# A state-space stage in a new order, its tables' products one tile later, and two transposes moved

## The chip, the cores and the metric

The kernel runs on one core of a Trainium2 chip. The metric is the device time of one execution in microseconds (us). Engines: PE (matmul), PEld (its weight loads), DVE, ACT, POOL, and SP, which in this kernel only issues DMAs.

## The reference, cut to what matters

A network on x of 512 tokens by 1024 features, in float32. First two blocks, each a token mixer (two branches of softmax attention, gated) and a feed-forward layer; then a block with a state-space mixer and a convolutional feed-forward layer; then one with stick-breaking attention and the same layer. The two parts that the change touches:

```python
def token_mixer(u, ...):
    ...
    ya = blocked_attention(qa, ka, va, 1.0 / math.sqrt(GQA_HEAD_DIM))
    ...
def s5_mixer(h, w_in, a_re, a_im, log_dt, b_re, b_im, c_re, c_im, d_skip, w_glu):
    u = (h @ w_in).astype(f32).reshape(bsz, seq, N_GROUPS, SSM_GROUP)
    ...
    bu_re = jnp.einsum('blgh,gph->blgp', u, bb_re)
    ...
    _, _, s_re, s_im = lax.associative_scan(combine, (a_seq_re, a_seq_im, bu_re, bu_im), axis=1)
    y = (jnp.einsum('blgp,ghp->blgh', s_re, c_re) - jnp.einsum('blgp,ghp->blgh', s_im, c_im)
         + d_skip.astype(f32) * u)
    y = jax.nn.gelu(y.reshape(bsz, seq, D_SSM))
    z = y @ w_glu
    return z[..., :D_MODEL] * jax.nn.sigmoid(z[..., D_MODEL:])
```

The operators ab, bb and f come from the parameters alone, not from x.

## The kernel before, in words

Activations lie transposed, 128 features by 512 tokens a tile. Each float32 operand is split into a high and a low part, and a product is three matmuls of 128x512 (`wh` with both parts of x, `wl` with the high one); a weight tile of 512 KB is loaded to `raw` by SP (L199) and split by ACT (`wh`, L238) and DVE (`wl`, L241 or L255). The time line: mixer 0, feed-forward 0, mixer 1 (to about 1120 us), feed-forward 1 (`ffn1`, to about 1545), the state-space stage (`ssm`, to about 1700), `ffn2`, stick attention, `ffn2`.

**Plan.** Each stage adds functions to a plan, whose items are run in turn and record instructions; a scheduler then sets each engine's order by its own estimates, except for what is pinned in the order of the program.

**Mixer 1.** The table `MIX` sets the order of items: `f` and `g` are pieces of projections (six matmuls), and for attention `aq` scores (`s`), `ae` exponentials (`p`, L827), `an` the scaling of `p` by its sum (DVE, L834), `at` four transposes (`pT`, L367) with `pt` copied by ACT (L847) and its low part taken by DVE (L848), `ap` the product with v (`o`). `mixer` moves two items of it for l = 1.

**Tables.** `ssm_gen` returns a list of functions that `ffn1` of l = 1 spreads evenly over its items. For each of 8 tiles of groups, `gen(i)` has: `fetch` (SP loads `g_c` and `g_b`), `bbar` (`g_bb`), `stacks` (`g_bs`, and `g_c` scaled and copied, L1465 to L1468), `expansion` twice (the products of c and of bb with powers of the transition: L1425, L1426, and the sums `go` and `gw`, L1430, all DVE), `table(i)` (`gt`, L1405 to L1409), `lags` (PE products of `g_bs` with `g_c` and `go` into `gps`, and the stores of `go` to `od` and `g_gs` to `gg`), `flip` (PE transposes of `gw`, the store to `wd`) and `spread` (eight copies from `gg` to `td`). So the stage's operators `od`, `td`, `wd` and tables `cd` lie in DRAM.

**State-space stage.** After three leading tiles of u, the table `ORDER` gives the order of everything; all of it is pinned, on every engine. `u3.0` to `u7.3` are pieces of six matmuls for the u tiles; for tile i: E takes u from PSUM (DVE), A stores it to `ud` on ACT's queue (L1548), D loads it back rearranged as `U` on SP's (L1552), w, x, b and o load `wt`, `tt`, `tab` and `ot` on SP's (L1556 to L1568), S are the states (`vps`, eight small products that the trace shows as 16 matmuls), V, R, C, X and Z rotate, scan and turn them, T and O are the lags and the outs (both into `yps`), G, g, H, I the gelu, J, Q, a, l the way of y through DRAM, and k the matmuls of w_glu. `hi`, `lo` and `raw` stand for a weight's split and load. A DMA issue on SP or ACT that has to wait holds back what stands behind it on that engine.

Of the kernel before, what the change touches and what calls it, by code (L numbers as in the profile page):

```python
# [52 lines left out]
for _name, _w in (("ident", 128), ("ones_d", 128), ("ones_q", 128), ("ones_kv", 128), ("blk", 128),  # L53
# [4 lines left out]


ORDER = """  # L60
    o1 u3.0 o0 o4 o2 u3.1 b1 b0 M0 b4 b2 u3.2 M1 E1 u3.3 E0 A1 E2 hi u4.0 A0 E3 A2 u4.1 lo A3 u4.2 raw D1 u4.3 D0 E4
    hi u5.0 D2 D3 lo A4 u5.1 raw S1 u5.2 V1 o3 D4 S0 R1 u5.3 V0 w4 C1 S2 hi R0 M3 X1 u6.0 o6 E5 V2 T1 C0 A5 R2 M2 u6.1
    o5 X0 S4 Z1 C2 b3 u6.2 V4 x4 D5 Z0 M4 T0 X2 lo b6 u6.3 w6 R4 raw T2 hi E6 u7.0 w5 C4 A6 S3 Z2 M6 X4 lo b5 u7.1 o7
    V3 Z4 raw O1 b7 u7.2 G1 R3 w7 O0 g1 D6 H1 I1 J1 u7.3 C3 G0 x6 T4 g0 hi x5 x7 E7 Q1 M5 lo H0 S6 A7 X3 I0 raw S5 J0
    Z3 a1 V6 l1 O4 V5 O2 G4 R6 g4 D7 H4 T3 I4 G2 Q0 J4 g2 H2 T6 R5 Q4 a0 O3 C6 C5 X6 l0 X5 Z6 S7 M7 G3 Z5 a4 T5 V7 l4
    g3 O6 R7 H3 I2 C7 J2 O5 G6 I3 X7 g6 Q2 J3 Z7 H6 I6 T7 G5 J6 g5 Q3 H5 k0 a2 I5 l2 J5 Q6 a3 O7 l3 Q5 a6 l6 k1 G7 g7
    a5 H7 l5 I7 k2 J7 k3 Q7 k4 a7 l7 k5 k6 k7
"""


# [38 lines left out]
class Kernel:  # L109
# [4 lines left out]
    V0 = 20  # L114
    VD = 1
    O1 = 1
    O2 = 1
    RP = True
    PA = True
    H0 = 17  # L120
    Q1 = 'scalar'
    Q2 = 'sync'
    Q3 = 'scalar'
    Q4 = 'sync'
# [15 lines left out]
    S1 = (2,4)  # L140
# [756 lines left out]
    def mixer(self, l, xs, st, nxt, mid, feed=None):  # L897
# [252 lines left out]
            ops[f"y{p}"] = (lambda p=p: reload_y(p)), ()  # L1150
        mix = MIX.split()
        if l == 1:
            for x, y in (("aq0", "f13"), ("ae0", "f14")):
                mix.remove(x)
                mix.insert(mix.index(y) + 1, x)
        for x in mix:
# [112 lines left out]
    def ssm_gen(self):  # L1269
# [6 lines left out]
        g = {}  # L1276
# [113 lines left out]
        def table(i):  # L1390

            box = {}
            sh = [128, 8, 8, 8]
            gs_ = slice(8 * i, 8 * i + 8)
            H = lambda z: g["hi" + z][:, :, gs_].rearrange("p j g -> p g j").unsqueeze(3).to_broadcast(sh)
            L = lambda z: g["lo" + z][:, :, gs_].rearrange("p k g -> p g k").unsqueeze(2).to_broadcast(sh)

            def part(k, a, b, op):
                def f():
                    if k == 0:  # L1400
                        box["t"] = self.s4("gt", F32)
                    o = box["t"][:, k].rearrange("p (g j k) -> p g j k", g=8, j=8)
                    w = self.s2("cx")
                    x = w.rearrange("p (g j k) -> p g j k", g=8, j=8)
                    v.tensor_tensor(o, H("r"), L(a), ALU.mult)  # L1405
                    v.tensor_tensor(x, H("i"), L(b), ALU.mult)
                    v.tensor_tensor(box["t"][:, k], box["t"][:, k], w, op)
                    if k == 1:
                        nc.sync.dma_start(self.Cd[i], box["t"])  # L1409
                return f  # L1410
            return [part(0, "r", "i", ALU.subtract), part(1, "i", "r", ALU.add)]

        def expansion(out, c1, c2, a):

            sh = [128, 4, 8, 16]
            C = lambda c, k: c()[:, 4 * k:4 * k + 4].unsqueeze(2).to_broadcast(sh)
            P = lambda n, k: g[n][:, a:a + 8, g["g0"] + 4 * k:g["g0"] + 4 * k + 4].rearrange("p d g -> p g d").unsqueeze(3).to_broadcast(sh)
            res = []
            for k in range(2):
                box = {}  # L1420

                def mul(k=k, box=box):
                    o = out()[:, 4 * k:4 * k + 4].rearrange("p g (d h) -> p g d h", d=8)
                    t = box["t"] = self.s2("cx").rearrange("p (g d h) -> p g d h", g=4, d=8)
                    v.tensor_tensor(o, C(c1, k), P("P1", k), ALU.mult)  # L1425
                    v.tensor_tensor(t, C(c2, k), P("P2", k), ALU.mult)  # L1426

                def add(k=k, box=box):
                    o = out()[:, 4 * k:4 * k + 4].rearrange("p g (d h) -> p g d h", d=8)
                    v.tensor_tensor(o, o, box["t"], ALU.add)  # L1430
                res += [mul, add]
            return res

        def gen(i):
            box = {}
            gs_ = slice(8 * i, 8 * i + 8)

            def fetch():
                g["g0"] = 8 * i
                c = box["c"] = T("g_c", [2, 8, 16], 2)  # L1440
                b = box["b"] = T("g_b", [2, 8, 16], 2)
                nc.sync.dma_start(c, self.ins["ssm_c"][i])
                nc.sync.dma_start(b, self.ins["ssm_b"][i])

            def bbar():

                b = box["b"]
                bb = box["bb"] = T("g_bb", [2, 8, 16], 2)
                x = T("g_x", [8, 16])
                y = T("g_y", [8, 16])  # L1450
                F = lambda n: g[n][:, gs_].unsqueeze(2).to_broadcast([128, 8, 16])
                v.tensor_tensor(bb[:, 0], b[:, 0], F("fr"), ALU.mult)
                v.tensor_tensor(x, b[:, 1], F("fi"), ALU.mult)
                v.tensor_tensor(bb[:, 1], b[:, 1], F("fr"), ALU.mult)
                v.tensor_tensor(y, b[:, 0], F("fi"), ALU.mult)
                v.tensor_tensor(bb[:, 0], bb[:, 0], x, ALU.subtract)
                v.tensor_tensor(bb[:, 1], bb[:, 1], y, ALU.add)

            def stacks():

                bb, c = box["bb"], box["c"]
                bs = box["bs"] = T("g_bs", [8, 16], 2)
                v.tensor_copy(bs[up], bb[up, 0])
                v.tensor_copy(bs[dn], bb[dn, 1])
                v.tensor_scalar(c[dn], c[dn], -1.0, None, ALU.mult)  # L1465
                c0 = box["c0"] = T("g_c0", [8, 16], 2)
                v.tensor_copy(c0[up], c[up, 0])
                v.tensor_copy(c0[dn], c[dn, 1])  # L1468
                box["o"] = self.s4("go", F32, [128, 8, 128])
                box["w"] = self.s4("gw", F32, [128, 8, 128])  # L1470

            def lags():
                o, c0 = box["o"], box["c0"]
                bs = box["bs"].rearrange("p g h -> p (g h)")
                nc.sync.dma_start(self.Od[i], o)
                ps = self.ps("gps")
                for q in range(4):
                    r = slice(32 * q, 32 * q + 32)
                    for two in range(2):
                        z = 128 * two  # L1480
                        self.mm(ps[r, z:z + 16], bs[:, r], c0[:, 2 * q + two], start=True, stop=True)
                        self.mm(ps[r, z + 16:z + 128], bs[:, r], o[:, 2 * q + two, 0:112], start=True, stop=True)
                gs = T("g_gs", [128], 2)
                par = self.const("par")
                nc.scalar.activation(gs, ps[:, 0:128], AF.Copy, scale=par[:, 0:1])
                v.scalar_tensor_tensor(gs, ps[:, 128:256], par[:, 1:2], gs, op0=ALU.mult, op1=ALU.add)
                dd = T("g_dd", [16])
                v.tensor_tensor(dd, g["d"][:, 16 * i:16 * i + 16], self.const("delta"), ALU.mult)
                v.tensor_tensor(gs[:, 0:16], gs[:, 0:16], dd, ALU.add)
                nc.sync.dma_start(self.Gd[i].rearrange("g h d -> (g h) d"), gs)  # L1490

            def spread():
                for j in range(8):
                    w = 128 - 16 * (7 - j)
                    nc.sync.dma_start(self.Td[i][16 * j:16 * j + 16, :, 128 - w:128],
                                      self.Gd[i][:, :, 0:w].rearrange("g h d -> h g d"))

            def flip():
                w = box["w"]
                wt = self.s4("gwt", F32, [128, 8, 128])  # L1500
                for k in range(2):
                    ps = self.ps("gps")
                    for q in range(4):
                        self.tr(ps[:, 128 * q:128 * q + 128], w[:, 4 * k + q], self.const("ident"))
                    nc.scalar.copy(wt[:, 4 * k:4 * k + 4].rearrange("p g d -> p (g d)"), ps)
                nc.sync.dma_start(self.Wd[i], wt)
            return ([fetch, bbar, stacks] + expansion(lambda: box["o"], lambda: box["c"][:, 0], lambda: box["c"][:, 1], 1)
                    + expansion(lambda: box["w"], lambda: box["bb"][:, 0], lambda: box["bb"][:, 1], 0) + table(i) + [lags, flip, spread])
        for i in range(8):
            ops += gen(i)  # L1510
        return ops

    def load_w(self, i):
        self.wt[i] = self.s4("wt", F32, [128, 8, 128])
        getattr(self.nc, self.LDQ).dma_start(self.wt[i], self.Wd[i])
# [708 lines left out]
```

## Time and profile before

| | us |
|---|---|
| three executions, median | 2752.75 (2751.21 to 2753.26) |
| the profiled execution | 2752.57 |
| its span | 2750.9 |
| outside the span | 1.7 |

The profile is of one execution. PE is the engine with the most busy time; the page gives, for the span in 40 slices, the clock that was granted to PE, which has two levels, 2.4 GHz (1.0) and 1.2 GHz (0.5), so a window's mean tells what share of it ran at the lower one. In a timeline a matmul's us is its run through the array, and the next begins before it ends; the pitch is read from the starts.

### The profile page before, as it was taken

Reading aid. Unit: us, or ns where it says so; the run is one execution under the profiler, and the core shown is the slowest. Engines: PE = TensorE matmul, PEld = TensorE weight load, DVE = VectorE, ACT = ScalarE, POOL = GpSimd, SP = SyncE. Lnnn points to the kernel's source line nnn. Section 1 sums busy time; section 2 is a strip of 40 time slices with the busy share of each in tenths; the row PEclk is TensorE's granted clock in tenths of the full one; section 3 lists DMA queues with packets and bytes.
Section 4 is the critical chain, followed back from the end, with each engine's and each line's share of the span. In section 5 each row is a group of like instructions: output and inputs, shape, how many; then the busy total and the mean of one; then the engine's idle time right before and its main releaser. Section 6 shows DMA issues by size and latency. Waiting matters only on the chain.

```text
span 2750.9 us, 35305 instructions
## 1 busy us (share of the span) xinstructions
PE 2687.3 (98%) x13474; PEld 2257.8 (82%) x13474; DVE 1849.5 (67%) x2942; ACT 1320.0 (48%) x2235; POOL 236.6 (9%) x242
## 2 busy tenths in 40 slices
PE   9999999999999999999999799999999999999998
PEld 7888888888877888878878698888887888888887
DVE  7889864444587897698964674656456777575554
ACT  6566554333465674533323353423236888532323
POOL 0000000000210100000001100101111111110101
PEclk9999999999999999999999899999999999999999
DMA  5323333333232324355545463333324223232331
GB/s 208 117 71 97 127 110 106 99 99 93 85 119 98 94 85 150 129 176 161 168 142 192 157 211 100 99 95 98 100 81 148 80 83 108 92 100 92 100 94 60
DMA packets 125818, 317.95 MB, mean 116 GB/s; under 512 B 36304, under 2 KB 43984, under 8 KB 125520
## 3 DMA queue, kind: packets, MB, share of 16 engines
q1 hardware_dynamic: 111872, 298.87, 33.7%
q0 software_dynamic: 2432, 7.34, 1.2%
q10 hardware_dynamic: 11344, 9.47, 1.1%
q8 instruction: 106, 1.74, 0.3%
q14 instruction: 64, 0.52, 0.1%
HBM read 264.78 MB, written 45.88 MB: 113 GB/s over the span
## 4 chain that ended last, share of the span: by engine, by line
PE 52%; ACT 5%; DVE 5%; issue 2%; DMA 1%; POOL 1%; SPq 0%; DVEq 0%; POOLq 0%; ACTq 0%
PE mm L348 46%; PE yps L348 2%; DVE wl L241 1%; PE s L348 1%; ACT e L1839 1%; PE o L348 1%; PE vps L348 1%; ACT wh L238 1%; ACT e L1838 1%; ACT e L1843 1%; ACT sp L395 0%; ACT whl L395 0%; ACT w L1859 0%; DVE e L1844 0%; PE z L348 0%
## 5 line engine op out<-in xcount | busy, mean ns | idle before, releaser
L348 PE MATMUL mm<-xg,wh 128*128 128x512 f32 (+1 forms) x4080 | 1223.2, 383 | 16.6 <-DVE xg L399 11.6
L348 PEld LDWEIGHTS mm<-xg,wh 128*128 128x128 f32 x4080 | 749.1, 189 | 168.3 <-DVE xg L399 16.8
L238 ACT ACTIVATE wh<-raw 128x1024 fp32r<-128x1024 f32 (+2 forms) x412 | 426.1, 1039 | 797.8 <-PE mm L348 539.7
L348 PE MATMUL mm<-xg,wl 128*128 128x512 f32 (+1 forms) x2024 | 763.8, 379 | 0.0
L241 DVE TENSOR_TENSOR wl<-raw,wh 128x1024 fp32r<-128x1024 f32 (+2 forms) x412 | 522.0, 1270 | 155.7 <-ACT wh L238 153.8
L348 PE MATMUL mm<-hid,wh 128*128 128x512 f32 (+1 forms) x1816 | 540.5, 381 | 0.7 <-DVE hid L396 0.4
L348 PEld LDWEIGHTS mm<-xg,wl 128*128 128x128 f32 x2024 | 383.7, 190 | 71.4
L348 PEld LDWEIGHTS mm<-hid,wh 128*128 128x128 f32 x1816 | 336.3, 189 | 67.1 <-DVE hid L396 1.4
L348 PE MATMUL mm<-hid,wl 128*128 128x512 f32 (+1 forms) x908 | 344.6, 380 | 0.0
L348 PE MATMUL mm<-yhl,wh 128*128 128x512 f32 x640 | 201.0, 394 | 0.0
L348 PEld LDWEIGHTS mm<-hid,wl 128*128 128x128 f32 x908 | 171.2, 189 | 32.2 <-issue 0.2
L453 POOL TENSOR_TENSOR acc<-acc,sq 128x512 f32<-128x512 f32 (+1 forms) x65 | 81.0, 1247 | 905.2 <-ACT sq L441 905.1
L348 PEld LDWEIGHTS mm<-yhl,wh 128*128 128x128 f32 x640 | 117.7, 188 | 22.8 <-ACT yhl L395 0.3
L1745 POOL TENSOR_TENSOR gt<-gt,cv 128x512 f32<-128x512 f32 x44 | 79.9, 1815 | 586.9 <-ACT wh L238 445.6
L348 PE MATMUL mm<-yhl,wl 128*128 128x512 f32 x320 | 125.1, 391 | 0.0
L1753 DVE SCALAR_TENSOR_TENSOR xr<-mm,xr 128x512 f32<-128x512 f32 (+1 forms) x50 | 33.5, 670 | 124.5 <-PE mm L348 124.5
L705 DVE TENSOR_TENSOR part<-part,mm 128x512 f32<-128x512 f32 (+1 forms) x52 | 33.5, 644 | 112.7 <-PE mm L348 112.7
L1733 DVE SCALAR_TENSOR_TENSOR gt<-mm,rr 128x512 f32<-128x512 f32 x88 | 60.4, 690 | 66.5 <-PE mm L348 66.4
L689 DVE SCALAR_TENSOR_TENSOR ht<-mm,rr 128x512 f32<-128x512 f32 x64 | 43.9, 688 | 89.5 <-PE mm L348 89.4
L820 DVE TENSOR_REDUCE nm<-s 128x1 f32<-128x512 f32 x128 | 86.5, 682 | 19.7 <-PE s L348 19.3
L847 ACT ACTIVATE pt<-pT 128x512 fp32r<-128x512 f32 x128 | 74.6, 593 | 47.3 <-PE pT L367 45.3
L827 ACT ACTIVATE p<-s,nm 128x512 f32<-128x512 f32 x128 | 87.0, 683 | 11.0 <-DVE nm L820 8.9
(321 smaller groups left out, 3435.3 us busy)
## 6 DMA issues: line engine op xcount, KB each, us to landing
raw<-in_w_up SPq DMA_DIRECT2D x152, 512.0 KB, 3.6
raw<-in_w_down SPq DMA_DIRECT2D x96, 512.0 KB, 3.6
raw<-in_w_in SPq DMA_DIRECT2D x51, 512.0 KB, 3.5
xd<-xr SPq DMA_DIRECT2D x16, 512.0 KB, 3.3
gd<-z SPq DMA_DIRECT2D x32, 256.0 KB, 2.2
g<-gd SPq DMA_DIRECT2D x32, 256.0 KB, 3.9
raw<-in_w_o SPq DMA_DIRECT2D x16, 512.0 KB, 3.6
raw<-in_w_glu SPq DMA_DIRECT2D x16, 512.0 KB, 4.4
```

Source lines behind the costliest of these rows:

```text
L238: ins = self.nc.scalar.activation(h, x, AF.Copy)
L241: ins = lo_engine.tensor_tensor(l, x, h.bitcast(F32), ALU.subtract)
L348: ins = self.nc.tensor.matmul(out, lhsT, rhs, **kw)
L453: eng.tensor_tensor(st["acc"][:, cols], st["acc"][:, cols], sq[:, cols], ALU.add)
L689: nc.vector.scalar_tensor_tensor(t, ps, 0.0, st["r"], op0=ALU.max, op1=ALU.mult)
L705: nc.vector.tensor_tensor(p, p, ps[:, cols], ALU.add)
L820: nc.vector.tensor_reduce(nm, ps, AX.X, ALU.max, negate=True)
L827: nc.scalar.activation(p, ps, AF.Exp, bias=nm, accum_out=sm)
L847: nc.scalar.activation(hi[:, :, q0:q0 + 128], v, AF.Copy)
L1733: v.scalar_tensor_tensor(t, ps, -0.5, st["r"], op0=ALU.mult, op1=ALU.mult)
L1745: nc.gpsimd.tensor_tensor(t, t, sg.pop(n), ALU.mult)
L1753: ins = v.scalar_tensor_tensor(x, ps[:, cols], 0.5, x, op0=ALU.mult, op1=ALU.add)
```

## The change

The table `ORDER` is replaced by another with the same operations. In the new one the u tiles are in natural order; the loads U of a tile come before any `ot` or `tab`, which are spread over the stage. In `mixer` for l = 1, the transposes at0 and at1 move behind f29 and f31. In `ssm_gen`, the fetch of tile i+1 stands before the expansions of tile i, `g["g0"]` is set in `bbar`, and lags, flip and spread of tile i stand behind `bbar` of tile i+1 (for the last tile, behind two empty functions). Lines behind the mixer's stay, those behind `ssm_gen`'s end are 2 higher.

```diff
 ORDER = """
-    o1 u3.0 o0 o4 o2 u3.1 b1 b0 M0 b4 b2 u3.2 M1 E1 u3.3 E0 A1 E2 hi u4.0 A0 E3 A2 u4.1 lo A3 u4.2 raw D1 u4.3 D0 E4
...
+    u3.0 u3.1 M0 u3.2 M1 E0 u3.3 E1 A0 E2 hi u4.0 A1 E3 A2 u4.1 lo A3 u4.2 raw D0 u4.3 D1 E4 hi u5.0 lo A4 D2 u5.1 D3
+    u5.2 raw u5.3 b0 b1 S0 E5 hi lo A5 u6.0 D4 V0 o0 b2 w4 T0 b3 u6.1 raw S1 R0 u6.2 V1 o1 C0 D5 S2 w5 R1 X0 x4 M2
...
 """
...
-            for x, y in (("aq0", "f13"), ("ae0", "f14")):
+            for x, y in (("aq0", "f13"), ("ae0", "f14"), ("at0", "f29"), ("at1", "f31")):
...
             def fetch():
-                g["g0"] = 8 * i
...
             def bbar():
 
+                g["g0"] = 8 * i
...
-            return ([fetch, bbar, stacks] + expansion(lambda: box["o"], lambda: box["c"][:, 0], lambda: box["c"][:, 1], 1)
-                    + expansion(lambda: box["w"], lambda: box["bb"][:, 0], lambda: box["bb"][:, 1], 0) + table(i) + [lags, flip, spread])
-        for i in range(8):
-            ops += gen(i)
+            return ([fetch], [bbar], [stacks], expansion(lambda: box["o"], lambda: box["c"][:, 0], lambda: box["c"][:, 1], 1)
+                    + expansion(lambda: box["w"], lambda: box["bb"][:, 0], lambda: box["bb"][:, 1], 0) + table(i), [lags, flip, spread])
+        gens = [gen(i) for i in range(8)]
+        ops[1:1] = gens[0][0]
+        for i, (_, bar, stack, mults, products) in enumerate(gens):
+            ops += bar + (gens[i - 1][4] if i else []) + stack + (gens[i + 1][0] if i < 7 else []) + mults
+        ops += [lambda: None] * 2 + gens[7][4]
         return ops
```

SP at the start of the state-space stage, before. Names end in the DRAM tensor's number: `od_79` is tile 0 of `od`, `cd_95` of `cd`, `ud_111` of `ud`.

```order
L199 DMA raw<-in_w_glu 128x1024 x3
L1564 DMA ot<-od_80 128x1024
L1564 DMA ot<-od_79 128x1024
L1564 DMA ot<-od_83 128x1024
L1564 DMA ot<-od_81 128x1024
L1568 DMA tab<-cd_96 128x1024
L1568 DMA tab<-cd_95 128x1024
L1568 DMA tab<-cd_99 128x1024
L1568 DMA tab<-cd_97 128x1024
L199 DMA raw<-in_w_glu 128x1024
L1552 DMA U<-ud_112 128x512
```

The same place with the change:

```order
L199 DMA raw<-in_w_glu 128x1024 x4
L1554 DMA U<-ud_111 128x512
L1554 DMA U<-ud_112 128x512
L1554 DMA U<-ud_113 128x512
L1554 DMA U<-ud_114 128x512
L199 DMA raw<-in_w_glu 128x1024
L1570 DMA tab<-cd_95 128x1024
L1570 DMA tab<-cd_96 128x1024
L1554 DMA U<-ud_115 128x512
L1566 DMA ot<-od_79 128x1024
L1570 DMA tab<-cd_97 128x1024
```

Four `ot` and four `tab` stood ahead of the first U; now only w_glu does, and `ot` of tile 0 comes behind five U.

DVE around tile 6 of the tables, in `ffn1`, before (`part` sums a down-projection tile, L705, `wl` splits a weight):

```order
L705 TENSOR_TENSOR part<-part,mm 128x512
L241 TENSOR_TENSOR wl<-raw,wh 128x1024
L705 TENSOR_TENSOR part<-part,mm 128x512
L241 TENSOR_TENSOR wl<-raw,wh 128x1024
L705 TENSOR_TENSOR part<-part,mm 128x512
L1465 TENSOR_SCALAR g_c<-g_c 64x256
L1467 COPY g_c_13105<-g_c 64x128
L1468 COPY g_c_13105<-g_c 64x128
L1425 TENSOR_TENSOR go<-g_c,g_P_11402 128x512
L1426 TENSOR_TENSOR cx<-g_c,g_P_11403 128x512
L1425 TENSOR_TENSOR go<-g_c,g_P_11402 128x512
L1430 TENSOR_TENSOR go<-go,cx 128x512
```

With the change:

```order
L1468 COPY g_c_13092<-g_c 64x128
L1488 TENSOR_TENSOR g_dd<-g_d,consts 128x16
L689 SCALAR_TENSOR_TENSOR ht<-mm,rr 128x512
L1425 TENSOR_TENSOR go<-g_c,g_P_11419 128x512
L241 TENSOR_TENSOR wl<-raw,wh 128x1024
L694 TENSOR_TENSOR hid<-hq,hid 128x512
L1426 TENSOR_TENSOR cx<-g_c,g_P_11420 128x512
L1425 TENSOR_TENSOR go<-g_c,g_P_11419 128x512
L1430 TENSOR_TENSOR go<-go,cx 128x512
L1426 TENSOR_TENSOR cx<-g_c,g_P_11420 128x512
L705 TENSOR_TENSOR part<-part,mm 128x512
L1430 TENSOR_TENSOR go<-go,cx 128x512
```

The g_c copies, the three `go` products and one sum of a tile stood behind the last of a row of `part`; they now stand ahead of the first, with `ht` and `hid` of the up-projection among them.

PE in mixer 1 around the first transposes, before:

```order
L348 MATMUL mm<-xg,wh 128x512 x2
L348 MATMUL mm<-xg,wl 128x512
L367 MATMUL pT<-consts,p 128x128 x4
L348 MATMUL s<-kk,qs 128x512 x4
L348 MATMUL mm<-xg,wh 128x512 x2
L348 MATMUL mm<-xg,wl 128x512
L348 MATMUL mm<-xg,wh 128x512 x2
L348 MATMUL mm<-xg,wl 128x512
L367 MATMUL pT<-consts,p 128x128 x4
L348 MATMUL mm<-xg,wh 128x512 x2
```

With the change, from the last six matmuls of a piece ahead of at1's transposes on:

```order
L348 MATMUL mm<-xg,wl 128x512
L348 MATMUL mm<-xg,wh 128x512 x2
L348 MATMUL mm<-xg,wl 128x512
L367 MATMUL pT<-consts,p 128x128 x4
L348 MATMUL mm<-xg,wh 128x512 x2
L348 MATMUL mm<-xg,wl 128x512
L348 MATMUL mm<-xg,wh 128x512 x2
L348 MATMUL mm<-xg,wl 128x512
L348 MATMUL o<-pt,vst 128x256
L348 MATMUL mm<-xg,wh 128x512 x2
L348 MATMUL mm<-xg,wl 128x512
L348 MATMUL mm<-xg,wh 128x512
```

at0's four `pT` stood ahead of the four `s` and now stand 16 matmuls lower; at1's now stand six matmuls ahead of the first `o`.

## Rows read from the trace of the kernel before

**Rows 1.** The page's first part: busy time and share of the span.
```profile
PE 2687.3 (98%) x13474; PEld 2257.8 (82%) x13474; DVE 1849.5 (67%) x2942; ACT 1320.0 (48%) x2235; POOL 236.6 (9%) x242
```

**Rows 2.** PE's waits over the span: line and tile <- what ended it: us, times, longest.
```profile
PE mm L348 <- DVE xg L399: 11.6, 14, 2.7
PE vps L348 <- DMA U<-ud: 10.1, 1, 10.1
PE gps L348 <- DVE go L1430: 5.5, 3, 2.4
PE pT L367 <- DVE p L834: 3.8, 2, 3.0
```

**Rows 3.** Busy time by window: us, engines (instructions), clock, DMA share, GB/s.
```profile
826.40:834.40 8.00, 4.99 (x20) 3.87 (x19) 7.93 (x16) 5.43 (x12) 0.00 (x0) 0.79 0.47 167
1219.30:1227.70 8.40, 6.00 (x48) 4.74 (x47) 8.40 (x14) 1.18 (x2) 0.00 (x0) 0.80 0.31 96
1388.50:1404.10 15.60, 9.44 (x53) 7.10 (x53) 15.23 (x25) 2.60 (x4) 0.00 (x0) 0.67 0.22 85
...
1560.80:1579.30 18.50, 8.36 (x39) 7.59 (x39) 4.33 (x5) 2.24 (x3) 0.00 (x0) 0.63 0.85 283
1579.30:1648.10 68.80, 68.80 (x548) 65.96 (x547) 50.04 (x70) 37.73 (x60) 0.00 (x0) 1.00 0.67 215
```

**Rows 4.** PE's timeline, state-space stage: start, us, instruction, [idle before <- releaser].
```profile
1559.92 0.39 PE L348 MATMUL mm<-xg,wl 128*128 128x512 f32 x1
...
1560.60 0.39 PE L348 MATMUL mm<-xg,wl 128*128 128x512 f32 x1
1571.13 3.68 PE L348 MATMUL vps<-U,wt 128*128 128x64 f32 x16 [10.14 <-DMA U<-ud]
```

**Rows 5.** Timelines of SP and of ACT: DMA issues of the state-space stage.
```profile
1548.68 1.85 SPq L1564 DMA_DIRECT2D ot<-od  x4
...
1564.10 2.34 SPq L1552 DMA_DIRECT2D U<-ud  x4
...
1552.48 0.38 ACTq L1548 DMA_DIRECT2D ud<-u  x1
```

**Rows 6.** DMA from 1545 to 1580: packets, MB; issues with KB, median us to landing.
```profile
DMA packets 7793, 9.46 MB, mean 270 GB/s; under 512 B 5488, under 2 KB 5488, under 8 KB 7792
...
q1 hardware_dynamic: 2592, 8.13, 63.4%
q10 hardware_dynamic: 5200, 1.31, 17.2%
...
ot<-od SPq DMA_DIRECT2D x5, 512.0 KB, 7.8
...
ud<-u ACTq DMA_DIRECT2D x5, 256.0 KB, 10.0
U<-ud SPq DMA_DIRECT2D x5, 256.0 KB, 7.2
```

**Rows 7.** The same from 1580 to 1590.
```profile
ot<-od SPq DMA_DIRECT2D x2, 512.0 KB, 3.8
...
ud<-u ACTq DMA_DIRECT2D x1, 256.0 KB, 3.2
```

**Rows 8.** DVE's timeline before and in tile 6 of the tables.
```profile
1377.87 0.69 DVE L705 TENSOR_TENSOR part<-part,mm 128x512 f32<-128x512 f32 x1 [3.30 <-PE mm L348]
...
1389.47 0.29 DVE L1465 TENSOR_SCALAR g_c<-g_c 64x256 f32<-64x256 f32 x1
```

**Rows 9.** DVE's timeline, tile 0 of the tables.
```profile
1221.19 1.27 DVE L1430 TENSOR_TENSOR go<-go,cx 128x512 f32<-128x512 f32 x2
...
1224.80 1.21 DVE L241 TENSOR_TENSOR wl<-raw,wh 128x1024 fp32r<-128x1024 f32 x1
```

**Rows 10.** DVE's timeline, mixer 1.
```profile
829.09 0.48 DVE L834 TENSOR_SCALAR p<-p,ri 128x512 f32<-128x512 f32 x1
...
833.47 1.28 DVE L820 TENSOR_REDUCE nm<-s 128x1 f32<-128x512 f32 x2
```

More of the change, by code (lines that the diff above doesn't have):

```diff
@@ L60 @@
 ORDER = """
-    o1 u3.0 o0 o4 o2 u3.1 b1 b0 M0 b4 b2 u3.2 M1 E1 u3.3 E0 A1 E2 hi u4.0 A0 E3 A2 u4.1 lo A3 u4.2 raw D1 u4.3 D0 E4
[L62 to L67, printed above, removed]
+    u3.0 u3.1 M0 u3.2 M1 E0 u3.3 E1 A0 E2 hi u4.0 A1 E3 A2 u4.1 lo A3 u4.2 raw D0 u4.3 D1 E4 hi u5.0 lo A4 D2 u5.1 D3
+    u5.2 raw u5.3 b0 b1 S0 E5 hi lo A5 u6.0 D4 V0 o0 b2 w4 T0 b3 u6.1 raw S1 R0 u6.2 V1 o1 C0 D5 S2 w5 R1 X0 x4 M2
+    u6.3 o2 V2 Z0 S3 hi E6 b4 C1 A6 u7.0 o3 V3 lo O0 X1 M3 Z1 raw R3 x5 u7.1 G0 b5 T1 R2 u7.2 C3 S4 g0 X3 C2 u7.3 o4
+    H0 Z3 M5 O1 D6 M4 w6 X2 I0 J0 Z2 hi lo T2 G1 V4 g1 raw S5 H1 E7 I1 A7 O2 o5 J1 R4 b6 x6 V5 T3 C4 G2 g2 M6 Q0 S6 R5
+    H2 w7 O3 o6 I2 X4 J2 Z4 T4 C5 V6 D7 a0 R6 T5 M7 Q1 l0 X5 O4 Q2 C6 G3 b7 Z5 x7 X6 g3 a1 k0 Z6 H3 G4 I3 a2 g4 J3 S7
+    l2 H4 l1 I4 O5 V7 o7 Q3 J4 R7 C7 T6 G5 g5 X7 Q4 T7 H5 Z7 a3 O6 I5 l3 J5 a4 l4 O7 G6 Q5 g6 H6 I6 J6 k1 G7 a5 g7 l5
+    H7 I7 Q6 k2 J7 k3 a6 Q7 l6 k4 a7 l7 k5 k6 k7
 """
```

## The prediction

> **What bounds the kernel now.** I read the page's first part, then PE's waits, then the windows around the long ones, then the timelines of the engine each of them names. PE is busy for 98% of the span [rows 1], so a change that only moves work can give back idle time and time at the lower clock, and nothing else. The waits [rows 2] show where idle time is. The largest, 11.6 us in 14 pieces for xg, lies at the stage boundaries, which this change leaves alone. Three others lie in stretches it touches: 10.1 us for one U load in the state-space stage, 5.5 us for `go` in the tables' background work, 3.8 us for the scaled `p` in mixer 1.
>
> The windows [rows 3] add the clock. Of a stretch whose mean clock is c, a share 2(1-c) ran at the lower level, 1.2 instead of 2.4 GHz; half of PE's busy time there is lost. Each fall came after a gap of 2.4 us or more in these four.
> - Mixer: 8.00 us, 4.99 busy, clock 0.79: 3.0 idle, 3.4 us slow, 1.7 lost in them. **Loss 4.7.**
> - Tile 0 of the tables: 8.40, 6.00 busy, 0.80: 2.4 idle, 3.4 slow, 1.7 lost. **Loss 4.1.**
> - Tile 6: 15.60, 9.44 busy, 0.67: 6.2 idle, 10.3 slow. Some 2.2 of the idle time falls into the slow part (that behind the first two gaps of 1.7 and 2.2), so 8.1 busy at half speed lose 4.0. **Loss 10.2.**
> - State-space: 18.50, 8.36 busy, 0.63: 10.1 idle, 13.7 slow, of them 6.8 idle and 6.9 busy, 3.4 lost. **Loss 13.6.**
>
> Together 32.6 us; nothing else in the span is touched. The profiled execution took 2752.57 us, 0.2 below the median of the runs shown, so its sum can be held against the median.
>
> **State-space stage: the loads' order.** PE ends its last due matmul about 1561.0 and starts the states of tile 1 at 1571.1 [rows 4], when its U has landed. Why so late? SP puts four 512-KB `ot` loads out from 1548.7 and U only from 1564.1 [rows 5], because U has to follow ACT's store of u, and that store flew about 10 us [rows 6], against 3.2 us for the same store when SP had less out [rows 7]. U then flew 7.2 us. Yet no `ot` is used before the first outs, more than 15 us later: from 1579.3 to 1648.1, where the last outs end, PE has no gap [rows 3].
>
> The new order puts nothing between the w_glu loads and the U loads. The store of u0 goes out where that of u1 did (1552.5 [rows 5]), lands at about 1555.8 with the 3.2 us of rows 7, and U0 goes out behind a w_glu load, which waits for DVE to finish an earlier w_glu tile: about 1557.1 by my walk, an estimate. With the loaded flight of 7.2 it lands at 1564.3; with the short one of the store, 1560.3. PE comes to states 0 at about 1563.6, since 12 more matmuls (the rest of u5, three in 0.68 us by the starts in rows 4) now stand ahead of them. So the wait is between 0 and 0.7; I take 0, as the engines have only w_glu and U to move then. What is late next are the eight `ot`, the tables and the last `wt` and `tt`, now issued among the U loads. I walked them by hand with flights of 3.5 to 6 us: the tightest is table 0, which comes as rotate 0 wants it (about 1566.5; DVE waits there, PE does not), then turn 0, 3 us ahead of outs 0. The other outs had 2.5 us or more. The same bytes move in either order. **Gain 13.6; bounds 4 (U as late as in the first rival) and 13.6.**
>
> **Tables: products one tile later.** `gen` now fetches a tile ahead and records the lags, the flip and the spread of a tile after the next tile's `bbar`. No instruction is added but two empty plan items; the same DMAs, matmuls and vector operations are issued. On DVE the g_c operations of tile 6 stood behind the fourth `part` and ran one after the other from 1389.5 with PE waiting, though DVE had been idle 3.3 us before each of the last three [rows 8] (one stands there). In the new order the last `go` sum stands behind the first of the four `part` (5.4 us before that row) and the last `gw` sum behind the second, the one of the row, while PE's lags move up by only 6 matmuls (1.4 us). So `go` is there by about 1376 and `gw` by about 1381; PE asks at 1387: **gain 10.2**, bounds 6.2 (the clock falls anyway) and 10.2. What covers these operations is DVE's idle time of 3.3 us per 5.4; four or five of 0.6 us go into each.
>
> At tile 0 DVE's order hardly changes, and PE comes later by 8 matmuls (1.8 us). The first `go` sum ended at 1221.86 [rows 9], PE now asks at 1221.3: 0.5 left. For the flip, one `wl` of 1.2 us now stands ahead of the last `gw` sum, which ends at about 1226.0 where PE asks about 1225.1: 0.9 left. Neither gap is near 2.4, so I let the clock stand: **gain 2.7**, bounds 1.0 (it falls) and 4.1. The other six tiles had no gap at all; their lags go between 6 matmuls up and 12 down the order, with the sums at least 31 matmuls (7 us) ahead: nothing, and in the worst case a gap or two of 1 us.
>
> **Mixer 1: transposes later.** The four pT of at0 move 16 matmuls (3.6 us) down, to 830.1; p was scaled at 829.6 [rows 10], so the 3.0-us gap goes. at1 now lies one group before ap0 uses it. DVE is the one that is late there: two maxima run from 833.5 to 834.8 in the old timing [rows 10]. In the new order they start up to 1.3 us sooner, without the pt between, and behind them come the low half of at0's pt, a scaling, a z and another `wl` (some 3.0 us in all) before the low half of at1's (0.7), which ends between 837.2 and 837.6. PE reaches its second o matmul at 836.0. A new gap of 1.5 us. **Gain 3.2**, bounds 1.5 (the clock falls after the new gap, 1.7) and 4.7 (DVE is in time). I take 3.2, for 1.5 is nearer to the gaps of about 1 us that kept the clock than to the 2.4 that lost it.
>
> **Sum:** 13.6 + 10.2 + 2.7 + 3.2 = 29.7, so 2752.6 - 29.7 = **2722.9 us**. With every lower bound it is 4 + 6.2 + 1.0 + 1.5 = 12.7 (2739.9), with every upper bound 32.6 (2720.0).
>
> **A rule weighed against the rows.** In the window of the long wait the loads' queue moved 8.13 MB in 2592 packets, 3.1 KB each, the stores' queue 1.31 MB in 5200, 0.25 KB each [rows 6]; the stores beside them took 10 us. The Trainium skill (DMA: Bandwidth & Descriptors, section Queues, rings and completion order) says that each DMA engine serves the queues it has work for in turn, a packet at a time. By that rule a store of small packets crawls whenever loads are queued at all, not only `ot` loads, and in the new order w_glu, the tables and the other U loads are still there; it would then come out as the first rival has it.
>
> **Rivals.**
> 1. *The stores of u stay slow.* Each keeps its 10 us though the `ot` loads are gone: u0 lands at 1562.6, U0 goes out then and lands at 1566.2 to 1569.8 (flights 3.6 and 7.2). PE waits 2.6 to 6.2 at states 0 and then runs at the lower clock, which costs 1.7 to 3.4 more: 4.3 to 9.6 given back, **2727 to 2733**. For it: the packets above. Against it: 3.2 us for a store with two `ot` loads in the same 10 us [rows 7]. By the rule of the Trainium skill above, this is what happens.
> 2. *The tables' gain does not come*: the earlier DVE work delays `wl` or `part`, on which every matmul group waits, and PE loses in small pieces what it gains at tiles 0 and 6: 12.9 given back, **2736**. Against it: DVE's idle 3.3 us in each group [rows 8].
> 3. *The transfers were the limit all along*: the change only moves the wait from U to the outs, whose `ot` and tables come last now; the 13.6 are given back at outs 0, **2736**. For it: 270 GB/s over the stage's first 35 us [rows 6]. Against it: the peak is past by 1579, DMA share 0.67 in the 69 us after [rows 3].
> 4. *Slower.* The `ot` load of a tile stands on SP, which issues in order, behind U loads that wait for stores and behind `tt` and `wt` loads that wait for PE; each comes late, PE waits at each of eight outs, and each wait takes the clock down (1.7). `ot` flew 7.8 us under load [rows 6] where I took 3.5 to 6; add one store's 10 us ahead of it in SP's queue and the 3 us of slack turn into some 3.4 late: 8 x (3.4 + 1.7) = 41, **2764**. It is slower than before once the eight come 2.0 us late each on average (8 x 3.7 = 29.7). Against it: six of the eight are issued after PE is done with the u tiles, when rows 3 show the engines a third idle.
> 5. *The order does not bite*: the recorded operations fall where they did. The order of SP, DVE and PE shows otherwise, in all three places.
>
> **How the numbers follow.** The forecast 0.55 (2719 to 2727), rival 1 0.18, rivals 2 and 3 0.08 each, rival 4 0.06 to over +0.2%, and 0.05 for a half-way form of 3 and 4 that lands near the old time. About 0.2% (5.5 us) can be told from no change. Faster 0.89, same 0.05, slower 0.06. The range: 2716, a little under all upper bounds, to 2740, which takes in rivals 1 to 3 and all lower bounds; the forecast's own range is 2719 to 2727.
>
> **What would show it.** Right: no PE wait for U over 1 us, states 0 near 1564, last gelu's matmuls end 13 us sooner; no slow stretch near 1393 and 1564; the waits for `go` under 1 us; a wait of about 1.5 us for pt in mixer 1 in place of 3.0 for p. Wrong: a wait for `ot` or `zx` at outs, the clock under 1.0 between 1580 and 1650, `ud` stores still near 10 us, or PE waits for `wl` between 1223 and 1540.

## The result, and the profile after

The changed kernel took 2723.62 us (median of 4, 2722.37 to 2725.27) against 2751.98 (median of 4) for the kernel before in the same series: ratio 0.9898, 95% interval 0.988 to 0.9915. The forecast was 2722.9. The profiled execution took 2722.47, its span is 2720.7.

The page's first part, which answers to [rows 1], and under it the waits of PE, which answer to [rows 2]:

```profile
PE 2674.5 (98%) x13474; PEld 2248.1 (83%) x13474; DVE 1852.8 (68%) x2942; ACT 1320.3 (49%) x2235; POOL 234.7 (9%) x242
```

```profile
PE mm L348 <- DVE xg L399: 11.9, 15, 2.6
...
PE o L348 <- DVE pt L848: 1.2, 1, 1.2
...
PE gps L348 <- DVE go L1430: 0.9, 1, 0.9
...
PE pT L367 <- DVE p L834: 0.8, 1, 0.8
...
PE gps L367 <- DVE gw L1430: 0.6, 1, 0.6
```

The 10.1 us for U are gone from the list; go went from 5.5 to 0.9, p from 3.8 to 0.8. New are 1.2 for pt and, at tile 0, 0.6 for gw, both forecast; the waits for gw in tile 6 (1.4 before) are gone. The 11.9 for xg is the boundaries' old share.

The windows of the same four places, and one behind them (us, busy time and instructions of PE, PEld, DVE, ACT and POOL, clock, DMA share, GB/s), which answer to [rows 3]:

```profile
825.60:836.90 11.30, 10.11 (x49) 7.82 (x47) 11.20 (x24) 8.49 (x17) 0.00 (x0) 1.00 0.52 170
1217.00:1223.00 6.00, 4.48 (x48) 3.62 (x48) 6.00 (x9) 1.40 (x2) 0.00 (x0) 1.00 0.42 123
1365.00:1390.00 25.00, 25.00 (x140) 20.62 (x139) 23.28 (x42) 5.58 (x7) 0.00 (x0) 1.00 0.54 161
1543.60:1562.00 18.40, 18.40 (x124) 16.68 (x123) 11.81 (x14) 9.01 (x14) 0.00 (x0) 1.00 0.92 333
1562.00:1620.00 58.00, 58.00 (x475) 56.16 (x475) 43.47 (x63) 31.33 (x51) 0.00 (x0) 1.00 0.76 256
```

Clock 1.00 in all of them, and in three no idle time at all. To see where the 30.2 us of span went, take four matmuls that mean the same in both traces, and the end: the restart after a wait for qs in mixer 1 (805.01 before, 804.16 after), after the wait for xg at the boundary to feed-forward 1 (1124.44, 1120.61), after the last wait for xg ahead of the state-space stage (1537.63, 1520.79), and after a wait of 0.2 us for hid in `ffn2` (2063.92, 2032.64).

| from one to the next | before, us | after, us | difference | forecast |
|---|---|---|---|---|
| start to mixer 1's scores | 805.01 | 804.16 | -0.9 | 0 |
| mixer 1, rest | 319.43 | 316.45 | -3.0 | -3.2 |
| feed-forward 1 with the tables | 413.19 | 400.18 | -13.0 | -12.9 |
| state-space stage and `ffn2` to that wait | 526.29 | 511.86 | -14.4 | -13.6 |
| to the end | 686.95 | 688.06 | +1.1 | 0 |

Some of this is luck of the clock. A wait of 1.44 us at the boundary near 737 was followed by a slow stretch of 3.4 us in the trace before, and by none after:

```profile
737.45 0.39 PE L348 MATMUL mm<-xg,wh 128*128 128x256 f32 x1 [1.44 <-DVE xg L399]
...
738.00:742.00 4.00, 4.00 (x23) 4.00 (x22) 3.93 (x8) 1.63 (x4) 2.32 (x3) 0.57 0.15 55
```

From this wait to mixer 1's scores it took 67.6 us in the eight traces of this document that have the slow stretch and 66.6 in the six that have none, which makes up the first row. The slow stretch at the start of the state-space stage was 6.8 us long before and 3.4 after; the run with the order table alone, which had the 6.8 too, took 512.69 us for the fourth row, so that row without this luck is -13.6. The last row's +1.1 has a wait of 1.7 us in stick attention that was 0.75 before, and a slow stretch behind it at 2216.7.

DMA of the stage's start, 1533 to 1547 (KB each, median us to landing), which answers to [rows 6]:

```profile
ud<-u ACTq DMA_DIRECT2D x5, 256.0 KB, 3.0
...
U<-ud SPq DMA_DIRECT2D x4, 256.0 KB, 4.7
tab<-cd SPq DMA_DIRECT2D x2, 512.0 KB, 6.1
```

PE at the first states of the stage:

```profile
1545.67 0.39 PE L348 MATMUL mm<-xg,wl 128*128 128x512 f32 x1
1545.90 1.89 PE L348 MATMUL vps<-U,wt 128*128 128x64 f32 x16
```

The median of five stores is 3.0 us where it was 10.0, that of four U 4.7 where it was 7.2. U0 went out at 1539.5 and landed at 1544.1; PE asked for it at 1545.9, behind a full row of matmuls.

While the first three stores flew, hardly any load did: the w_glu load ahead of them had landed at 1535.0, and SP issued the next at 1539.1. From 1535 to 1539 only the stores' queue moved data (packets, MB, share of 16 engines):

```profile
q10 hardware_dynamic: 2768, 0.70, 84.5%
```

DVE in tile 6 of the tables, which answers to [rows 8]: the first of the four `part`, the last `go` sum just behind it, and the last `gw` sum.

```profile
1366.67 0.68 DVE L705 TENSOR_TENSOR part<-part,mm 128x512 f32<-128x512 f32 x1
1367.26 0.68 DVE L1430 TENSOR_TENSOR go<-go,cx 128x512 f32<-128x512 f32 x1
...
1374.78 0.68 DVE L1430 TENSOR_TENSOR gw<-gw,cx 128x512 f32<-128x512 f32 x1
```

The sums end at 1367.9 and 1375.5; PE's products of them run from 1380.9 on without a gap. In mixer 1, where DVE was to be late, its timeline shows the weight split and the low half of at1's pt, whose end at 836.8 releases PE's second o matmul:

```profile
834.97 1.22 DVE L241 TENSOR_TENSOR wl<-raw,wh 128x1024 fp32r<-128x1024 f32 x1
836.11 0.69 DVE L848 TENSOR_TENSOR pt<-pT,pt 128x512 fp32r<-128x512 f32 x1
```

### The profile page after: what moved, and what is told of

Read it like the earlier page. It is cut to its first block, busy times and chain, and to the rows that moved or that the text cites. A ratio compares the mean times of both kernels' runs of the same rounds, so it can differ in the third digit from the quotient of the medians.

```text
span 2720.7 us, 35299 instructions
## 1 busy us (share of the span) xinstructions
PE 2674.5 (98%) x13474; PEld 2248.1 (83%) x13474; DVE 1852.8 (68%) x2942; ACT 1320.3 (49%) x2235; POOL 234.7 (9%) x242
## 4 chain that ended last, share of the span: by engine, by line
PE 52%; DVE 6%; ACT 4%; issue 1%; DMA 1%; POOL 0%; SPq 0%; DVEq 0%; POOLq 0%; ACTq 0%
PE mm L348 47%; PE yps L348 2%; PE z L348 1%; DVE wl L241 1%; PE o L348 1%; PE s L348 1%; PE vps L348 1%; ACT e L1841 0%; PE pT L367 0%; ACT e L1845 0%; ACT sp L395 0%; ACT e L1840 0%; ACT w L1861 0%; ACT whl L395 0%; DVE xg L399 0%
## 5 line engine op out<-in xcount | busy, mean ns | idle before, releaser
L348 PE MATMUL mm<-xg,wh 128*128 128x512 f32 (+1 forms) x4080 | 1219.4, 382 | 17.7 <-DVE xg L399 11.9
L705 DVE TENSOR_TENSOR part<-part,mm 128x512 f32<-128x512 f32 (+1 forms) x52 | 33.4, 642 | 92.0 <-PE mm L348 91.9
```

The lines of the kernel that those rows point to most:

```text
L348: ins = self.nc.tensor.matmul(out, lhsT, rhs, **kw)
L705: nc.vector.tensor_tensor(p, p, ps[:, cols], ALU.add)
```

## The experiments

All times are medians; the kernel before took between 2750.7 and 2752.5 in these series.

| run | us | ratio to before (95%) |
|---|---|---|
| order table alone | 2737.70 | 0.9948 (0.9934 to 0.9963) |
| tables' change alone | 2737.31 | 0.9946 (0.9931 to 0.9961) |
| mixer's change alone | 2747.91 | 0.9989 (0.998 to 0.9998) |
| four ot first | 2725.61 | 0.9903 (0.9885 to 0.9922) |
| four ot, four tab first | 2735.38 | 0.9938 (0.9923 to 0.9953) |
| before, eight loads later | 2750.64 | 0.9995 (0.9985 to 1.0004) |
| before, loads spread | 2775.79 | 1.009 (1.0075 to 1.0105) |
| early fetch alone | 2724.28 | 0.9902 (0.9887 to 0.9916) |
| late products alone | 2725.64 | 0.991 (0.9893 to 0.9926) |
| at1 earlier | 2721.86 | 0.9889 (0.9875 to 0.9904) |
| changed kernel again | 2723.29 | 0.9894 (0.9879 to 0.9908) |
| U5 late | 2746.98 | 0.9987 (0.9977 to 0.9997) |

### The three parts alone

Edits: the kernel before with only the new `ORDER`; with only the new `ssm_gen`; with only the new pairs in `mixer`.

> The kernel before with the new ORDER table alone. By the forecast's first term the stage gives back its 10.1 us wait for U and 3.4 us at the lower clock: 13.6 less than before, about 2738.5; u stores fly about 3 us, no slow stretch near 1560, the tables' and mixer's waits as before. If the transfers were the limit all along (third rival), the wait moves to the outs and the time stays within 3 us of before.

> The kernel before with the change to the tables' background work alone. By the second and third terms 10.2 + 2.7 = 12.9 less than before, about 2739; no wait for go in tile 6, some 1.5 us left at tile 0, the wait of 10 us for U still there. If the vector work only moves and delays weight splits (second rival), the time is within 3 us of before and PE waits for wl or wh appear between 1223 and 1540.

> The kernel before with the two moved transposes alone. By the last term 3.2 less than before, about 2749: the 3.0 us wait for p and the slow stretch of 3.4 us go, a wait of 1.2 us for pt comes. If the gap that takes its place lowers the clock as the old one did, 1.5 less (2750.5).

Measured against 2750.69 in the same series: -13.0, -13.4 and -2.8, together -29.2, where the forecast had 13.6, 12.9 and 3.2, and the whole change gave 28.4 in its own series and 29.2 in the repeat (2752.45 to 2723.29). So the parts add, within the noise. The mixer's 2.8 is the least sure by time alone (its interval is 0.5 to 5.5 us); the traces bear it out: the second row of the table above took 318.9 to 319.6 us in the five traces without the moved transposes and 316.0 to 316.8 in eight of the nine with them (317.9 in the run with the mixer's change alone, which has a slow stretch at 1048). Waits of PE in the run with the tables' change alone:

```profile
PE vps L348 <- DMA U<-ud: 9.5, 1, 9.5
...
PE gps L348 <- DVE go L1430: 0.9, 1, 0.9
```

go is down to the 0.9 of the changed kernel while the wait for U is there nearly as before (9.5 and 10.1): the two hardly touch each other. The third rival falls with the first run.

### Which loads made U late?

Edit to the changed kernel (the four also go from their later places):

```diff
-    u3.0 u3.1 M0 u3.2 M1 E0 ...
+    o0 o1 o2 o3 u3.0 u3.1 M0 u3.2 M1 E0 ...
```

> The changed kernel with the loads o0, o1, o2, o3 put back to the head of ORDER and nothing else moved. If big loads ahead in SP's queue are what slows the stores of u, these fly 8 to 10 us again, U0 lands at about 1549 to 1553 where PE asks at 1546, PE waits 3 to 7 us and loses another 1.7 to 3.4 at the lower clock: 2728 to 2734. If it was the order of the u tiles or of the tab loads that mattered, the stores stay near 3 us and the time within 2 us of the changed kernel (2722 to 2726).

It came out at 2725.6, within what the other side gave, while the stores are slow as on the first. DMA from 1531 to 1548:

```profile
ud<-u ACTq DMA_DIRECT2D x5, 256.0 KB, 7.6
...
U<-ud SPq DMA_DIRECT2D x3, 256.0 KB, 3.7
```

The stores are slow again (7.6 us; 3.0 without the ot). But U0 went out the moment u0 had landed, at 1543.5, and flew 4.3 us, and PE waited 0.9. The old wait needed more than stores of 7.6 us. So the four tab loads were put back too:

```diff
-    u3.0 u3.1 M0 u3.2 M1 ...
+    o0 o1 o2 o3 u3.0 u3.1 b0 b1 M0 b2 b3 u3.2 M1 ...
```

> The changed kernel with both o0 to o3 and b0 to b3 ahead of the first U, as in the kernel before. With the four ot alone the stores flew 7.6 to 8.7 us and PE waited 0.9. If the tab loads between the stores and U are the other half of the old wait (U goes out later and then flies 7 us, not 4.3), U0 lands 5 to 8 us after PE asks, the clock falls, and the time is 2731 to 2736. If four loads ahead or eight are the same, it stays within 2 us of the run with four (2725.6).

2735.4, the first side: 12.1 us over the changed kernel in the same series, most of the old loss, with U's wait of 7.8 and a slow stretch of 10.2 us. DMA from 1530 to 1556, PE's wait, and a wait of SP:

```profile
ot<-od SPq DMA_DIRECT2D x4, 512.0 KB, 8.4
tab<-cd SPq DMA_DIRECT2D x4, 512.0 KB, 5.9
...
ud<-u ACTq DMA_DIRECT2D x6, 256.0 KB, 9.8
U<-ud SPq DMA_DIRECT2D x5, 256.0 KB, 6.5
```

```profile
PE vps L348 <- DMA U<-ud: 7.8, 1, 7.8
...
SPq L1570 <- DMA ud<-u: 5.5, 1, 5.5
```

With eight loads ahead the stores are at 9.8 us again. SP held the third tab load until the store of u0 had landed, at 1544.9; so two tab and a w_glu load went out just ahead of U, which flew 6.5. The loss is steep: 0.9 us of wait with four loads ahead, 7.8 with eight. The tab loads without the ot were not tried, so it is not shown whether their place right ahead of U or the number of loads makes the difference.

### Is it enough to move these loads back?

Edit to the kernel before: `b1 b0 b4 b2 o1 o0 o4 o2` taken from the head of its `ORDER` and put behind `D3`.

> The kernel before with four ot and four tab loads (o1 o0 o4 o2, b1 b0 b4 b2) moved behind its first four U loads, and nothing else. If the loads in front of the stores and of U were the cause, the stores of u fly about 3 us, U1 lands at about 1560 where PE asks at 1561, and at least 8 of the 13 us come back: 2738 to 2743, a little more than the new table's 2737.7 as the table of tile 1 may now be late. If the natural order of the u tiles or the spread of the later loads is needed, PE still waits over 6 us at its first states: 2746 to 2751.

The stores flew 3.0 us and the first states waited 0.8, as expected on the first side; the time was 2750.6, as on the other, and neither had said why. PE's waits in the stage:

```profile
PE vps L348 <- DMA wt<-wd: 5.8, 1, 5.8
PE vps L348 <- DMA U<-ud: 0.8, 1, 0.8
```

The lump of eight loads now stands ahead of `wt` of tile 4, which flew 10.0 us; PE waited 5.8 for it and the clock stayed low for 13.7 us. The wait was moved, not removed. (The time is the same as before within its interval.) Then the loads were spread by hand (tab in twos, w4 ahead of the second two, each ot shortly before its outs; the u order as before):

> The kernel before with the same u order and steps, but its tab, ot and w4 loads spread: two tab behind the first four U, w4 ahead of the other two, each ot shortly before its outs. With eight loads moved in one lump the first states waited 0.8 us but a wt load 10 us behind them then cost 5.8 and a slow stretch. If the spread is the other half, no wait over 1.5 us is left and the stage gives back what the new table did: 2737 to 2742. If the natural order of the u tiles is needed too, a wait of over 3 us stands somewhere in the stage: 2745 to 2751.

2775.8, 23.7 slower than before, and far from both. PE's waits in the stage, windows ahead of the second wait to end, behind it, and from 2.4 us behind the first w_glu matmul on, and that matmul:

```profile
PE vps L348 <- DVE zx L1611: 5.3, 1, 5.3
PE vps L348 <- DMA U<-ud: 1.1, 1, 1.1
```

```profile
1579.30:1600.90 21.60, 21.60 (x161) 20.19 (x159) 16.41 (x22) 11.32 (x17) 0.00 (x0) 1.00 0.90 335
1606.30:1666.60 60.30, 60.30 (x278) 59.82 (x279) 22.79 (x33) 17.03 (x29) 0.00 (x0) 0.50 0.32 104
1666.70:1686.00 19.30, 19.30 (x103) 16.57 (x102) 3.37 (x5) 2.76 (x5) 0.00 (x0) 1.00 0.16 42
...
1664.28 1.20 PE L348 MATMUL mm<-yhl,wh 128*128 128x512 f32 x2
```

One wait of 5.3 us, which ended at 1606.3; then 60.3 us in which PE was busy without a gap at the lower clock; and full speed from 1666.7, 2.4 us after it got matmuls of 512 columns again. That is about 30 us lost to the clock on top of the wait.

The profile puts the wait down to a turned zx, which DVE ended at 1606.24. But the states that waited, first those of tile 6, take U and wt and no zx, and the U of tile 6 landed at 1606.17: its store had taken 11.6 us from 1584.7, and SP issued it behind four other loads, to fly 8.0.

```profile
1598.14 0.70 SPq L1552 DMA_DIRECT2D U<-ud  x1
...
ud<-u ACTq DMA_DIRECT2D x1, 256.0 KB, 11.6
...
U<-ud SPq DMA_DIRECT2D x1, 256.0 KB, 8.0
```

So PE could not have started sooner even without the zx: it is again a late U behind a slow store, at a later tile. This run does not say whether the natural order of the u tiles is needed: the hand-made spread brought a stall of its own. That stays open.

### What does one late load cost?

Edit to the changed kernel; PE's order is the same:

```diff
-    ... o1 C0 D5 S2 w5 ...
+    ... o1 C0 S2 w5 ...
...
-    ... V4 g1 raw S5 ...
+    ... V4 g1 raw D5 S5 ...
```

> The changed kernel with one load, U5, issued just ahead of its states instead of some 20 us before; PE's order is the same. It goes out at about 1577.8 and lands at 1582 to 1583, where PE asks at 1578.4: one wait of about 4 us in the stretch where PE has only the narrow products of the stage (64 columns) until the first w_glu matmuls, 20 us later. If the price of a stall is the one of the forecast's fourth rival (the wait and one slow stretch, 1.7 lost), the time is 2729 to 2731. If the clock stays low as long as PE gets narrow products alone, as it did for 61 us in the run with spread loads, the 20 us of work up to the w_glu matmuls take twice as long: 4 + 17 to 20, 2744 to 2748.

2747.0, the second side. PE's timeline and two windows:

```profile
1576.11 1.95 PE L348 MATMUL yps<-U,tt 128*128 128x64 f32 x16
1583.45 3.64 PE L348 MATMUL vps<-U,wt 128*128 128x64 f32 x16 [5.39 <-DMA U<-ud]
1586.88 3.62 PE L348 MATMUL yps<-vz,ot 128*128 128x63 f32 x16
1590.30 3.62 PE L348 MATMUL yps<-zx,ot 128*128 128x63 f32 x16
...
1620.98 1.20 PE L348 MATMUL mm<-yhl,wh 128*128 128x512 f32 x2
```

```profile
1570.00:1579.00 9.00, 8.06 (x66) 7.66 (x65) 6.71 (x10) 7.80 (x12) 0.00 (x0) 1.00 0.90 313
1583.50:1607.00 23.50, 23.50 (x111) 23.50 (x111) 8.10 (x12) 7.76 (x13) 0.00 (x0) 0.50 0.63 209
```

The same groups of 16 small matmuls in the changed kernel, at 1.79 us each:

```profile
1578.38 1.95 PE L348 MATMUL vps<-U,wt 128*128 128x64 f32 x16
1580.16 1.95 PE L348 MATMUL yps<-vz,ot 128*128 128x63 f32 x16
1581.95 1.95 PE L348 MATMUL yps<-zx,ot 128*128 128x63 f32 x16
```

With the late load they are 3.41 us apart, for the 37.5 us until the next matmuls of 512 columns, though PE never idles in them. The wait of 5.4 itself is the smaller part of what the run lost on the changed kernel: 23.4 us by the two medians, 24.5 with each held against the kernel before in its own series.

### Which half of the tables' change does it?

Edits to the changed kernel: the products back behind their own table, with the early fetch kept; and each fetch back ahead of its `bbar`, with the late products kept.

```diff
-            ops += bar + (gens[i - 1][4] if i else []) + stack + (gens[i + 1][0] if i < 7 else []) + mults
-        ops += [lambda: None] * 2 + gens[7][4]
+            ops += bar + stack + (gens[i + 1][0] if i < 7 else []) + mults + products
```

> The changed kernel with the fetch a tile ahead kept, but lags, flip and spread of a tile back behind its own table. On DVE the go sums of tile 6 then still stand behind the first part, 67 matmuls ahead of PE. If the early fetch alone moved them, no wait in tile 6 and only tile 0 loses, as PE's lags come six matmuls sooner: a wait for go of 1.5 to 2.3 there, 2724 to 2727. If the later products were what freed PE, the waits of tile 6 return: 2732 to 2735.

```diff
-        ops[1:1] = gens[0][0]
...
-            ops += bar + (gens[i - 1][4] if i else []) + stack + (gens[i + 1][0] if i < 7 else []) + mults
+            ops += gens[i][0] + bar + (gens[i - 1][4] if i else []) + stack + mults
```

> The changed kernel with the products a tile later kept, but each fetch back ahead of its own bbar. The go sums of tile 6 stand 67 matmuls ahead of PE here too. If the list's new spacing is enough, no wait in tile 6, at tile 0 a wait for go of 0.9 and none for gw: 2722 to 2725. If the fetch is needed, DVE waits for g_c and g_b in front of bbar, part and wl are late behind it, and tile 6 or others lose over 5 us: 2728 or more.

Each half alone takes all of tile 6's waits away, 2724.3 and 2725.6, which cannot be told from the whole. Waits for `gps` with the early fetch alone:

```profile
PE gps L348 <- DVE go L1430: 2.3, 1, 2.3
```

That is tile 0, 2.3 us, and the clock did not fall behind it, so even the worse place of tile 0 cost only the wait. With the late products alone the wait there is 0.8, and one of 1.2 for hid stands near 1268. In both runs the g_c operations of tile 6 stand ahead of the first `part` (from 1360.7 and 1365.6; that `part` runs at 1366.9 and 1369.4), where they stood behind the last. So tile 6's trouble reads as an accident of how the list fell on `ffn1`'s items, since either shift ends it.

### at1 one piece earlier

Edit to the changed kernel: `("at1", "f31")` becomes `("at1", "f30")`.

> The changed kernel with at1 behind f30 instead of f31, six matmuls earlier. DVE's low half of at1's pt then stands ahead of the z and the weight split that delayed it, so the wait of 1.2 us for pt in mixer 1 goes and nothing else changes: 1.2 less than the changed kernel, about 2722.4. If p of at1 or ACT's copy is late instead, a wait for p or for ACT's pt of 1 us or more stands there and the time is the same.

> The changed kernel once more, for the same chip and hour as the others: 2722 to 2726, with the wait of 1.2 us for pt in mixer 1.

```profile
PE o L348 <- DVE pt L848: 0.4, 1, 0.4
```

The wait is 0.4 where it was 1.2. The medians are 2721.86 and 2723.29, but the four times of the first (2720.40 to 2724.44) enclose those of the second (2723.13 to 2723.66), so 0.8 us of wait is shown and a gain of time is not. Nor do the traces show one: from the scores to the boundary mixer 1 took 316.14 us in the first and 316.00 in the second, where a later wait for ACT's pt was 2.0 us and 1.1.

## Why the prediction was right, and where its working was not

- **State-space term, 13.6.** Right in size (13.0 alone, 13.6 in the trace with like clocks) and in its cause, the stores and U behind big loads. The wait was put between 0 and 0.7; U was 1.8 us early, as it flew 4.5 and not the 7.2 taken from the loaded row. The working named the four ot alone; with these alone put back PE waited 0.9, and 7.8 once the tab loads stood there too.
- **Tables, 10.2 and 2.7.** Right: 13.0 by the traces, 13.4 alone. The gaps left at tile 0 were put at 0.5 and 0.9 and were 0.9 and 0.6, with the clock up. The early fetch and the late products were costed as one; each would have done for tile 6.
- **Mixer, 3.2.** Right in size: 3.0 and 2.8. The new gap is 1.2, not 1.5: with the 0.9 us by which this trace runs ahead there, DVE finished at 837.7 of the old timing (walked: 837.2 to 837.6) and PE asked at 836.5 (walked: 836.0).
- **Which gaps cost the clock.** Here the working was lucky. It says that each of the four falls came after a gap of 2.4 us or more; at tile 6 the gaps ahead of the fall at 1393.6 were shorter, 0.2 us apart:

```profile
1390.41 0.21 PE L348 MATMUL gps<-g_c,g_bs 128*32 128x16 f32 x2 [1.70 <-DVE g_c L1468]
1392.85 0.38 PE L348 MATMUL gps<-go,g_bs 128*32 128x112 f32 x2 [2.23 <-DVE go L1430]
```

And the same trace has the wait of 1.44 us near 737 with a fall behind it, nearer to the 1.5 expected in mixer 1 than any gap that was weighed. The new gap kept the clock in all eight traces that have it, but the length of a gap does not settle it: a wait of 1.2 us for xg ahead of the state-space stage was followed by a slow stretch in two of fourteen traces, and one of 1.1 us for U in the run with spread loads.
- **First rival, and the rule on queues.** The first three stores of the changed kernel took 2.7 to 3.0 us with hardly a load in flight. The fourth took 3.5 and the fifth 5.2, with w_glu and four U loads beside them, and the sixth, among tab, ot and wt loads, 12.0, when PE had no need of it. So the rival failed because SP had hardly anything out when the stores that count flew; that a store stays fast beside loads is not shown. The Trainium skill (DMA: Bandwidth & Descriptors, section Queues, rings and completion order) has each DMA engine serve in turn, a packet at a time, the queues that it has work for. The traces agree that loads on SP's queue slow ACT's stores; in which turns the packets go they do not show.
- **Second rival.** It did not come: between 1223 and 1505 PE waited 0.4 us for a late `hid`, and for no `wl` or `part`.
- **Third rival.** As put, it fell. But the run with eight loads moved in one lump is it at another place: the wait went from U to a wt.
- **Fourth rival, its price.** This is the step that was wrong. Each wait was priced at itself and 1.7 us of clock, and eight were thought needed. A single late load cost 23 to 25 us, most of what the change gives, and a single wait in the run with spread loads about 35: the clock stood at 0.50 for as long as the stage had narrow products alone. The chance given to slower, 0.06, rested on the number eight; by these prices two such waits would have done. (Its 8 x 3.7 is 29.6, not 29.7, which changes nothing.)

## What to carry to other kernels

A load on the critical path was late here for what was queued ahead of it and beside the store that feeds it, on another queue; list what is in flight when the store and the load go, and move behind them what is needed last. Then walk every load and store that comes after: a lump passed the wait on to a wt, and a spread by hand passed it on to the U of a later tile. Price a stall by what PE runs next: ahead of narrow products alone, one wait of 5 us cost 23 us and more in two runs here. When a background list causes a wait, see first where its items fell among the others; here either of two shifts was enough.

## What the hardware did that was not expected

At 2.4 GHz a stretch of narrow products alone kept its clock in the changed kernel: 58.0 us behind 1562 at 1.00, of them 25 us (1573 to 1598) without one matmul of 512 columns. Once the clock had fallen, the same products, back to back, were not seen to bring it up: 60.3 us at 0.50 in one run, 37.5 in another, PE busy throughout; it came back about 2.4 and 3.1 us after the first matmuls of 512 columns. The Trainium skill (TensorE: Matmul & The Clock Gate, section Part 1: The HAM clock gate) has a busy PE released to the full clock; these rows differ from it, and the measurement decides.

A wait of 2.4 us at tile 0 lowered the clock in all five traces that have it, and one of 2.3 there did not; the wait of 1.44 us near 737 lowered it in eight of fourteen traces, at 1.0 us each time.

A store of 256 KB in packets of 0.25 KB nearly fills the DMA engines by itself: from 1535 to 1539 of the changed kernel the stores alone moved 175 GB/s, with the engines 84.5% busy.
